# Attention of a first block regrouped over head pairs, and its first projections loaded raw through SyncE's queue

## The chip, the core and the metric

The kernel runs on one core of a Trainium2 chip. The metric is the device time of one execution in microseconds. The core has five instruction streams that this document names: TensorE (PE, matmuls; PEld is its weight load), VectorE (DVE), ScalarE (ACT), GpSimd (POOL, which here mostly issues DMAs) and SyncE (SP, which only issues DMAs). Matmuls read SBUF and write PSUM, which is held as eight buffers of 128 x 512 floats.

## The reference

The reference runs a two-layer "first block" and then a two-layer second block on 512 tokens of width 1024. Only the first block is touched. Cut to what matters, one layer of it is:

```
h = rmsnorm(x) ; z = h @ w_in                 # 1024 -> 1280 columns: fourier, 8 q heads, 2 k, 2 v heads, 4 memory q heads
y_f = real(fft2(z_fourier)) @ w_fourier       # 256 columns
q, k = rope(zq), rope(zk)
y_a = softmax(q k^T / 8 + window mask, with a sink logit) @ v      # |i - j| <= 128, 8 heads on 2 kv heads
km, vm = split(rmsnorm(mem) @ w_mem_kv)       # 256 memory tokens
y_m = softmax(zm km^T / 8) @ vm               # 4 heads
y = concat(rmsnorm(y_f), rmsnorm(y_a), rmsnorm(y_m)) @ w_out
x = x + rmsnorm(y)
x = x + rmsnorm((silu(h2 @ w_gate) * (h2 @ w_up)) @ w_down)        # h2 = rmsnorm(x), width 2816
```

All of it is in float32. The kernel gets float32 accuracy from fp32r matmuls by splitting each operand into a rounded high part and a remainder.

## The kernel before, in words

**Data.** Activations are feature-major: a tile holds 128 features by 512 tokens. A product of split operands is three matmuls (`mm3`, line 713: high times low, low times high, high times high). A weight tile of 1024 x 128 is loaded in two halves of 128 x 512 (`halves`, line 692): a DMA on POOL's queue writes the rounded high part, an engine writes its negative (`scale` by -1), and a second DMA on POOL's queue adds the original to it, so that the remainder is left. One output tile of a projection is 8 `mm3`, 24 matmuls of 512 columns. Everything in SBUF that matters here takes one of 100 slots of 128 x 512 floats (`NSLOT`), and a PSUM tile takes one of the eight buffers.

**The order of instructions** is worked out on the host. The program first records every operation in program order (`Plan.record`); `Plan.schedule` (line 423) then places them on the five engines by a model of their durations: each engine takes, of the operations that the model says are ready, the one that is needed earliest in TensorE's program order, up to 120 us ahead. Transfers are modelled as one queue in which all DMAs run one after the other (`state["dma"]`, lines 569 to 576). Each engine then runs its list strictly in that order on the chip. An operation that opens a tile earlier than program order would is only placed if no point of the program in between is filled up (`room`, line 465; `load` counts the tiles that are live at each point of the program order, and `self.low` is the first operation not yet placed):

```
if op.index > self.low and load[k][self.low:op.index].max() + n > self.cap[k] - min(self.MARGIN.get(k, 0), int(ahead / self.PACE)):
    return False
```

For PSUM the cap is 8 and the margin 0.

**A layer of the first block** (`block1`, line 1107) does this. `enter` (line 838) splits the eight tiles of x, times the gain, into high and low parts and sums their squares; the norm's factor itself (`late`, the tile `rb`) is worked out behind the first four projections and multiplied into their results. The ten projections (`project`, by `linear`, line 734) are recorded as tiles 4 (k), 0 (q), 5 (v), 1 (q) first, then 2 and 3, 6 and 7, 8 and 9 between the attention parts (0 to 3 are pairs of q heads, 6 and 7 the memory queries, 8 and 9 the fourier part). A tile below 5 gets rope in `ev` (line 1112): four DMAs on SP's queue shift blocks of 32 partitions, and three VectorE operations combine the tile with its shifted copy.

The attention of a head (`attend`, line 1064) has two parts. The first writes four score tiles (a block of 128 queries each, against two or three blocks of keys; two of 256 and two of 384 columns), three matmuls each with a contraction of 64, and the softmax on them. The second transposes the probabilities 128 x 128 at a time through TensorE, splits them, and multiplies them with the values. `run` (line 1159) records the first part of both heads of a pair, then a set of projections, then the second parts of both heads. Memory attention follows for its two pairs. After it, `group` normalises the three groups, each before its split, the fourier group last and by the other form of norm (`wide`, line 819), and the output projection runs its eight tiles one after another, 24 matmuls each.

In layer 0 `mem_in`, `mem_k`, `mem_v` (memory norm, keys and values) and `four_fold` (a small product of the channel transform with the fourier weights) are recorded between these parts; for layer 1 memory keys and values are worked out around layer 0's feed-forward part. In the first layer `linear` runs the four first projections one after the other; in the second it runs them in two halves of the tokens (`first=4`).

## Time and profile before

| | us |
|---|---|
| median of 3 runs | 3524.22 |
| lowest, highest | 3521.81, 3525.62 |
| the profiled execution | 3527.36 |
| its span (first to last instruction) | 3525.2 |
| TensorE busy in it | 3446.0 |

The profile is of one execution. TensorE's column counts a matmul as busy from its issue to its modelled end, at either clock, so 98% busy doesn't say that it ran at its full rate. Every operation has the line 646, because the plan issues them all from there; they are told apart by their tiles: `ps` is PSUM, `s` the slots, `in_...` tensors in memory. The shape of a matmul is written as contraction*columns of the stationary operand, then the moving operand: `128*128 128x512` is a projection, `64*128 64x256` a score tile, `128*64` a product with the values, and `ident` marks a transpose.

### The profile page before, as it was taken

The numbers are of one execution on the slowest core, as the hardware profiler recorded it, in microseconds if no ns is written. First come the engines' busy times: TensorE is split into PE (matmuls) and PEld (weight loads), VectorE is DVE, ScalarE is ACT, GpSimd is POOL, SyncE is SP. The second block draws the span as 40 slices with busy tenths as digits, with TensorE's granted clock in tenths as the row PEclk, the third lists the DMA queues.
The fourth block names the chain that finished last, engine by engine and source line by source line (L and its number), as shares of the span: only waits on it lengthen the run. The fifth ranks groups of instructions, "written<-read, shape, count | busy, mean of one in ns | idle before, by whom it ended". The sixth has DMA issues, their size and how long they took to land.

```text
span 3525.2 us, 44631 instructions
## 1 busy us (share of the span) xinstructions
PE 3446.0 (98%) x16280; PEld 2869.9 (81%) x16280; DVE 1941.6 (55%) x3942; ACT 882.9 (25%) x1709; POOL 1756.8 (50%) x2447
## 2 busy tenths in 40 slices
PE   7899999889999999999999999999999999999998
PEld 6688888768888988887888888888888888888887
DVE  6875432687342553339997444335333899844332
ACT  3642000364000211015733110011001574411000
POOL 5155454535446464653365544655465436654462
PEclk9899999889999999999999999999999999999999
DMA  9278797848779797996699977999799769998794
GB/s 251 60 175 192 158 202 153 202 105 172 165 156 218 170 218 162 220 218 128 131 220 229 235 158 158 216 198 203 159 215 218 139 121 228 214 238 170 161 199 107
DMA packets 361596, 638.02 MB, mean 181 GB/s; under 512 B 40736, under 2 KB 64032, under 8 KB 361376
## 3 DMA queue, kind: packets, MB, share of 16 engines
q0 software_dynamic: 349056, 616.75, 81.8%
q1 hardware_dynamic: 12320, 18.42, 1.6%
q8 instruction: 128, 2.10, 0.2%
q14 instruction: 92, 0.75, 0.1%
HBM read 626.10 MB, written 6.29 MB: 179 GB/s over the span
## 4 chain that ended last, share of the span: by engine, by line
PE 91%; DVE 4%; DMA 2%; issue 2%; ACT 0%; POOL 0%; SPq 0%; POOLq 0%; DVEq 0%; ACTq 0%
PE ps L646 91%; DVE s L646 4%; DMA s<-in_b_in 1%; ACT s L646 0%; POOL s L646 0%; DMA s<-in_a_in 0%; DMA s<-in_c_chan 0%; DMA s<-in_x 0%; DVE mx L646 0%; POOL rinv L646 0%; DVE sp L646 0%; SPq L646 0%; DVE rc L646 0%; DVE nb L646 0%; DVE sums L646 0%
## 5 line engine op out<-in xcount | busy, mean ns | idle before, releaser
L646 PE MATMUL ps<-s 128*128 128x512 f32 (+2 forms) x15706 | 3381.5, 376 | 45.2 <-DVE s L646 26.2
L646 PEld LDWEIGHTS ps<-s 128*128 128x128 f32 (+1 forms) x15706 | 2796.3, 188 | 602.9 <-issue 30.5
L646 POOL DMA_DIRECT2D s<-in_b x1088 | 786.3, 1028 | 667.9 <-DVE s L646 296.6
L646 ACT ACTIVATE s<-s 128x512 fp32r<-128x512 f32 (+3 forms) x716 | 404.6, 601 | 1737.5 <-DVE s L646 1128.4
L646 DVE TENSOR_TENSOR s<-ps,s 128x512 f32<-128x512 f32 (+4 forms) x642 | 397.8, 636 | 637.5 <-PE ps L646 631.8
L646 DVE TENSOR_SCALAR s<-s 128x512 fp32r<-128x512 f32 (+2 forms) x845 | 341.3, 423 | 471.5 <-DMA s<-in_b 278.5
L646 POOL DMA_DIRECT2D s<-in_a_f x544 | 396.9, 1082 | 348.4 <-DVE s L646 163.2
L646 DVE TENSOR_TENSOR s<-s 128x512 f32<-128x512 f32 (+2 forms) x822 | 500.3, 624 | 54.8 <-ACT s L646 33.3
L646 POOL DMA_DIRECT2D s<-in_b_in x368 | 287.8, 1008 | 266.7 <-ACT s L646 88.7
L646 DVE SCALAR_TENSOR_TENSOR s<-s,vecs 128x256 fp32r<-128x256 f32 (+25 forms) x446 | 287.9, 678 | 6.3 <-ACT s L646 3.2
L646 ACT ACTIVATE s<-s,vecs 128x512 f32<-128x512 f32 (+2 forms) x213 | 135.7, 656 | 310.2 <-DVE s L646 297.4
L646 POOL DMA_DIRECT2D s<-in_a_out x64 | 48.5, 994 | 156.5 <-PE ps L646 100.7
L646 DVE SCALAR_TENSOR_TENSOR s<-ps,s 128x512 f32<-128x512 f32 (+1 forms) x33 | 22.2, 674 | 183.0 <-PE ps L646 183.0
L646 ACT ACT_TABLE_LOAD x67 | 86.0, 1283 | 55.8 <-DVE s L646 47.9
L646 ACT ACTIVATE s<-ps 128x512 f32<-128x512 f32 (+1 forms) x40 | 21.3, 534 | 269.2 <-PE ps L646 245.7
L646 PE MATMUL ps<-ident,s 128*128 128x128 f32 x392 | 68.9, 307 | 20.0 <-DVE s L646 14.4
L646 DVE RECIPROCAL s<-s 128x128 f32<-128x128 f32 (+1 forms) x48 | 83.1, 1741 | 8.3 <-ACT s L646 8.2
L646 DVE CAST s<-s 128x512 fp32r<-128x512 f32 (+1 forms) x190 | 81.9, 431 | 6.8 <-DMA s<-in_pos 1.2
L646 ACT ACTIVATE s<-s,nb 128x256 f32<-128x256 f32 (+3 forms) x128 | 70.5, 552 | 44.9 <-DVE nb L646 43.4
L646 PEld LDWEIGHTS ps<-ident,s 128*128 128x128 f32 x392 | 53.0, 157 | 33.8 <-DVE s L646 15.3
L646 POOL TENSOR_TENSOR rinv<-rms,nhalf 128x2 f32<-128x2 f32 (+1 forms) x17 | 17.3, 1015 | 117.0 <-DVE rms L646 109.0
L646 POOL DMA_DIRECT2D s<-in_a_in x80 | 58.8, 884 | 24.9 <-DMA s<-in_a_in 13.1
(71 smaller groups left out, 874.1 us busy)
## 6 DMA issues: line engine op xcount, KB each, us to landing
s<-in_b POOLq DMA_DIRECT2D x1024, 256.0 KB, 6.5
s<-in_a_f POOLq DMA_DIRECT2D x512, 256.0 KB, 6.3
s<-in_b_in POOLq DMA_DIRECT2D x368, 256.0 KB, 6.4
s<-in_a_in POOLq DMA_DIRECT2D x80, 256.0 KB, 7.6
s<-in_a_out POOLq DMA_DIRECT2D x64, 256.0 KB, 7.4
s<-in_b_out POOLq DMA_DIRECT2D x64, 256.0 KB, 7.6
s<-in_b POOLq DMA_DIRECT2D x64, 128.0 KB, 6.3
s<-in_b_mo POOLq DMA_DIRECT2D x32, 256.0 KB, 5.9
```

Of the source, the lines that this page charges most:

```text
L646: getattr(getattr(nc, op.eng), op.fn)(*[real(v) for v in op.args], **{k: real(v) for k, v in op.kw.items()})
```

## The change

Five things change in the first block.

1. Attention is recorded as separate steps for a pair of heads: `scores` writes the eight score tiles of both heads, alternating between the heads matmul by matmul; `turn` transposes and splits one head's probabilities; `apply` multiplies with the values. `ask(p)` is scores and softmax of pair p, `answer` is `turn`, `put` is `apply`. Scores of pair p+2 are recorded behind the last product of pair p. Pairs 4 and 5 are the memory heads.
2. The other matmuls (projections 2, 3, 6, the memory keys and values in layer 0, projections 7, 8, 9, `four_fold`, fourier) are a generator, `fillers`, from which `pull(us)` records a given amount of TensorE work between the steps. It stops right behind a matmul, so that a projection's PSUM tile can be open, its evacuation not yet recorded, when the next step is recorded.
3. In layer 0 the first four projections are recorded by `open`: raw float32 halves come by one DMA each on SP's queue and are split by ScalarE or VectorE; all four tiles take contraction steps 0 to 3 first and 4 to 7 after that.
4. The three group norms all use the form with the narrow sums (`inv` and `bcast`), in steps (`Group`) that are recorded apart.
5. The output projection opens five tiles at once, over the window heads' four steps first, then the fourier steps, then the memory steps; the other three tiles follow as before.

`mem_k`, `mem_v` and `fourier` become generators that yield between their matmuls; the plan, its model and its limits are as before.

```diff
+    def scores(self, heads, rng):
+        mm = self.nc.tensor.matmul
+        S = [[] for _ in heads]
+        for i in range(4):
+            a, b = rng[i]
+            cols, kc = slice(128 * i, 128 * i + 128), slice(128 * a, 128 * b)
+            for t in S:
+                t.append(self.ps()[:, :128 * (b - a)])
+            for n, (x, y) in enumerate(((0, 1), (1, 0), (0, 0))):
+                for t, (q, k, (lo, hi)) in zip(S, heads):
+                    mm(t[i], q[x][lo:hi, cols], k[y][lo:hi, kc], start=n == 0, stop=n == 2)
+        return S
...
+    def turn(self, P, rng, order):
+        nc = self.nc
+        out = []
+        for kb in order:
+            qs = [i for i in range(4) if rng[i][0] <= kb < rng[i][1]]
+            q0, q1 = 128 * qs[0], 128 * (qs[-1] + 1)
+            pt = self.ps()[:, :q1 - q0]
+            for j, i in enumerate(qs):
+                off = 128 * (kb - rng[i][0])
+                nc.tensor.transpose(pt[:, 128 * j:128 * j + 128], P[i][:, off:off + 128], self.ident)
+            h, l = self.t(F32R)[:, :q1 - q0], self.t(F32R)[:, :q1 - q0]
+            self.split(pt, h, l)
+            out.append((kb, slice(q0, q1), h, l))
+        return out
...
+    def apply(self, turned, V, vcols, y, yrows):
+        po = self.ps()[0:64]
+        for n, (kb, q, h, l) in enumerate(turned):
+            self.mm3(po[:, q], V[0][kb][:, vcols], V[1][kb][:, vcols], h, l, n == 0, n == len(turned) - 1,
+                     skip_group_check=True)
+        self.nc.copy(y[yrows[0]:yrows[1]], po)
...
+    def steps(self, srcs, acts, evac):
+        kt = len(acts)
+        for m, src in enumerate(srcs):
+            ps = self.ps()
+            w = {}
+            for k in range(kt):
+                if k // 8 not in w:
+                    w[k // 8] = self.wload(src[k // 8])
+                wh, wl = w[k // 8]
+                self.mm3(ps, wh[:, k % 8], wl[:, k % 8], acts[k][0], acts[k][1], k == 0, k == kt - 1)
+                yield 0.68
+            evac(m, ps)
+    def open(self, srcs, acts, evac):
+        nc = self.nc
+        pss = [self.ps() for _ in srcs]
+        for c in (0, 4):
+            for m, src in enumerate(srcs):
+                raw, h, l = (self.t(dt).rearrange("p (k c) -> p k c", c=128) for dt in (F32, F32R, F32R))
+                nc.sync.dma_start(out=raw, in_=src[0][:, c:c + 4])
+                self.split(raw, h, l)
+                for k in range(4):
+                    self.mm3(pss[m], h[:, k], l[:, k], acts[c + k][0], acts[c + k][1],
+                             c + k == 0, c + k == KD - 1)
+        return lambda: [evac(m, ps) for m, ps in enumerate(pss)]
...
+    class Group:
+        def __init__(self, net, l, ys, ks, acts):
+            self.net, self.l, self.ys, self.ks, self.acts = net, l, ys, ks, acts
+            self.s = net.squares(ys)
+        def rms(self):
+            self.r = self.net.inv([self.s], 128 * len(self.ys))
+        def finish(self):
+            net = self.net
+            rb = net.bcast(self.r)[1]
+            for k, y in zip(self.ks, self.ys):
+                net.tt(y, rb, out=y)
+                self.acts[k] = net.split_gain(y, net.vec(f"g_grp{self.l}", k))
...
-        project([4, 0, 5, 1], hold=4, before=late, first=4 if l else 0)
+        src = lambda ms: [[I[f"a_in{l}"][m]] for m in ms]
+        ms = [4, 0, 5, 1]
+        if l == 0:
+            done = self.open(src(ms), a, lambda i, ps: ev(ms[i], ps))
+            late()
+            done()
+        else:
+            self.linear(src(ms), a, lambda i, ps: ev(ms[i], ps), hold=4, before=late, first=4)
...
+        near = [(0, 2), (0, 3), (1, 4), (2, 4)]
+        every = [(0, 2)] * 4
...
-        run(window(0, ya[0]), lambda: project([2, 3]))
-        if l == 0:
-            self.mem_in()
-        run(window(1, ya[1]), lambda: project([6, 7]))
-        run(window(2, ya[2]), lambda: project([8, 9]))
-        if l == 0:
-            self.four_fold()
-        run(window(3, ya[3]), lambda: (self.mem_k(0), self.mem_v(0)) if l == 0 else None)
-        run(memory(0, ym[0]))
-        run(memory(1, ym[1]))
-        acts = []
-        def group(ys):
-            rb = self.norm(ys, 128 * len(ys), wide=self.W[1 + len(acts) // 3])
-            for y in ys:
-                self.tt(y, rb, out=y)
-                acts.append(self.split_gain(y, self.vec(f"g_grp{l}", len(acts))))
-        group(ya)
-        group(ym)
-        group(self.fourier(l, [z[8], z[9]]))
+        acts = {}
+        def fillers():
+            rest = [2, 3, 6]
+            yield from self.steps(src(rest), a, lambda i, ps: ev(rest[i], ps))
+            if l == 0:
+                self.mem_in()
+                yield 0.0
+                yield from self.mem_k(0)
+                yield from self.mem_v(0)
+            last = [7, 8, 9]
+            yield from self.steps(src(last), a, lambda i, ps: ev(last[i], ps))
+            if l == 0:
+                self.four_fold()
+            yield from self.fourier(l, [z[8], z[9]])
+        fill = fillers()
...
+        def pull(us):
+            for cost in fill:
+                us -= cost
+                if us <= 0:
+                    break
+        def ask(p):
+            if p < 4:
+                S = self.scores([(z[p], z[4], r) for r in rows], near)
+                return [self.softmax(S[u], 0.125, (self.vec(f"sink{l}", p + 4 * u), nsink[:, p + 4 * u:p + 4 * u + 1]),
+                                     mask) for u in range(2)]
+            t = p - 4
+            S = self.scores([(z[6 + t], self.km[t], r) for r in rows], every)
+            return [self.softmax(S[u], 0.125) for u in range(2)]
+        def answer(p, P, u):
+            if p < 4:
+                return self.turn(P[u], near, [0, 3, 1, 2])
+            return self.turn(P[u], every, [0, 1])
+        def put(p, turned, u):
+            if p < 4:
+                self.apply(turned, z[5], slice(64 * u, 64 * u + 64), ya[p], rows[u])
+            else:
+                hd = 2 * (p - 4) + u
+                self.apply(turned, self.vm, slice(64 * hd, 64 * hd + 64), ym[p - 4], rows[u])
+        P = {0: ask(0)}
+        pull(5.4)
+        P[1] = ask(1)
+        pull(5.4)
+        groups = {}
+        for p in range(6):
+            t0 = answer(p, P[p], 0)
+            if p == 4:
+                groups[0] = self.Group(self, l, ya, range(4), acts)
+            pull(1.3)
+            t1 = answer(p, P[p], 1)
+            if p == 4:
+                groups[0].rms()
+            put(p, t0, 0)
+            pull(1.3)
+            if p == 4:
+                groups[0].finish()
+            put(p, t1, 1)
+            if p < 4:
+                P[p + 2] = ask(p + 2)
+                pull(3.3 if l else 5.3)
+            del P[p]
+        pull(100.0)
+        groups[1] = self.Group(self, l, self.yf, (6, 7), acts)
+        groups[2] = self.Group(self, l, ym, (4, 5), acts)
         ev, post = self.keep(f"g_post{l}")
-        self.linear([[I[f"a_out{l}"][m]] for m in range(KD)], acts, ev, last=2, done=post)
+        outs = [I[f"a_out{l}"][m] for m in range(KD)]
+        n = 5
+        first = [0, 1, 2, 3]
+        w = [self.wload(outs[m]) for m in range(n)]
+        full = [self.ps() for _ in range(n)]
+        def add(m, ks):
+            for k in ks:
+                self.mm3(full[m], w[m][0][:, k], w[m][1][:, k], acts[k][0], acts[k][1], k == 0, k == 5)
+        for m in range(n):
+            add(m, first)
+            if m == 1:
+                groups[1].rms()
+                groups[2].rms()
+            if m == 2:
+                groups[1].finish()
+                groups[2].finish()
+        for m in range(n):
+            add(m, [6, 7])
+        for m in range(n):
+            add(m, [4, 5])
+            ev(m, full[m])
+        self.linear([[outs[m]] for m in range(n, KD)], [acts[k] for k in range(KD)],
+                    lambda m, ps, c=ALL: ev(m + n, ps, c), last=2, done=post)
...
@@ mem_k and mem_v: after each mm3 @@
+                yield 0.36
@@ fourier: after each token block, and after each table of a token block @@
+            yield 0.7
...
-        return ys
+        self.yf = ys
```

## Rows read from the trace of the kernel before

**Rows 1.** The page: span, TensorE's busy time, and the chain that ended last.
```profile
span 3525.2 us, 44631 instructions
PE 3446.0 (98%) x16280; PEld 2869.9 (81%) x16280; DVE 1941.6 (55%) x3942; ACT 882.9 (25%) x1709; POOL 1756.8 (50%) x2447
...
PE 91%; DVE 4%; DMA 2%; issue 2%; ACT 0%; POOL 0%; SPq 0%; POOLq 0%; DVEq 0%; ACTq 0%
```
**Rows 2.** Windows by stage: start:end, length, busy us (instructions), clock, DMA share, GB/s.
```profile
0.00:22.09 22.09, 0.79 (x1) 0.32 (x2) 12.38 (x25) 11.12 (x17) 11.11 (x24) 1.00 1.01 308
20.00:46.00 26.00, 23.91 (x98) 20.23 (x99) 25.34 (x47) 10.60 (x16) 19.28 (x26) 1.00 1.18 289
31.40:83.90 52.50, 52.36 (x237) 43.26 (x236) 30.31 (x55) 10.62 (x21) 26.48 (x34) 1.00 1.05 236
83.90:198.20 114.30, 94.88 (x564) 75.43 (x565) 99.13 (x288) 72.46 (x202) 29.74 (x47) 0.87 0.34 78
620.70:652.60 31.90, 28.45 (x209) 27.59 (x208) 22.67 (x63) 10.66 (x28) 24.62 (x35) 0.89 1.12 271
652.60:685.60 33.00, 33.00 (x148) 27.06 (x147) 16.68 (x23) 9.33 (x14) 19.11 (x25) 1.00 1.14 254
685.60:788.70 103.10, 84.23 (x472) 65.38 (x472) 89.89 (x253) 62.50 (x177) 28.14 (x45) 0.82 0.40 90
```
**Rows 3.** Windows of the stretches in which the granted clock fell, one per layer.
```profile
83.90:143.00 59.10, 44.26 (x224) 33.31 (x224) 50.26 (x158) 35.16 (x98) 1.65 (x4) 0.77 0.05 14
685.60:738.20 52.60, 37.78 (x175) 30.01 (x174) 42.39 (x126) 24.08 (x70) 2.66 (x5) 0.64 0.17 41
```
**Rows 4.** Timeline of the start: start, length, instructions, idle before and its releaser.
```profile
15.05 0.72 ACT L646 ACTIVATE s<-s,first 128x512 fp32r<-128x512 f32 x1 [0.94 <-DMA s<-in_x]
22.09 9.06 PE L646 MATMUL ps<-s 128*128 128x64 f32 x31 [13.30 <-DMA s<-in_c_chan]
```
**Rows 5.** Timeline of VectorE and SyncE's queue around the ropes of both layers.
```profile
44.42 1.89 DVE L646 TENSOR_TENSOR s<-ps,s 128x512 f32<-128x512 f32 x3
45.14 2.53 SPq L646 DMA_DIRECT2D s<-s  x4
50.80 2.42 SPq L646 DMA_DIRECT2D s<-s  x4
73.58 2.02 DVE L646 TENSOR_TENSOR s<-s 128x512 f32<-128x512 f32 x3
...
661.60 3.08 DVE L646 TENSOR_TENSOR s<-ps,s 128x512 f32<-128x512 f32 x5
662.43 18.59 SPq L646 DMA_DIRECT2D s<-s  x20
687.36 2.01 DVE L646 TENSOR_TENSOR s<-s 128x512 f32<-128x512 f32 x3
```
**Rows 6.** DMA issues of the rope's shifts: count, KB each, median us to landing.
```profile
s<-s SPq DMA_DIRECT2D x40, 64.0 KB, 6.4
```
**Rows 7.** The loads of x: issue time ns (min/median/max), first and last start us.
```profile
L646 SPq DMA_DIRECT2D s<-in_x x8: 418/444/804, 1.2 to 5.0; - x8
```
**Rows 8.** Groups on VectorE in the first 46 us: splits of a 512-wide half.
```profile
L646 DVE TENSOR_SCALAR s<-s 128x512 fp32r<-128x512 f32 x12 | 4.9, 429 | 4.0 <-DMA s<-in_a_in 4.0
L646 DVE TENSOR_TENSOR s<-s 128x512 fp32r<-128x512 f32 x2 | 1.4, 687 | 0.0
```
**Rows 9.** Groups on TensorE by form: a projection's matmul, busy and mean ns.
```profile
L646 PE MATMUL ps<-s 128*128 128x512 f32 x13210 | 3027.7, 390 | 8.4 <-DVE s L646 8.4
```
**Rows 10.** Timeline of score matmuls: eight and three of one head; ten, partly two heads.
```profile
164.94 1.22 PE L646 MATMUL ps<-s 64*128 64x256 f32 x8
165.75 0.98 PE L646 MATMUL ps<-s 64*128 64x256 f32 x10
766.80 0.62 PE L646 MATMUL ps<-s 64*128 64x256 f32 x3
```

More of the change, by code (lines that the diff above doesn't have):

```diff
@@ L1129, in ev @@
                 z[m] = self.split_t(t)
-        def project(ms, **k):
-            self.linear([[I[f"a_in{l}"][m]] for m in ms], a, lambda i, ps: ev(ms[i], ps), **k)
-        project([4, 0, 5, 1], hold=4, before=late, first=4 if l else 0)
+        src = lambda ms: [[I[f"a_in{l}"][m]] for m in ms]
[6 more added lines that the diff above has]
+            self.linear(src(ms), a, lambda i, ps: ev(ms[i], ps), hold=4, before=late, first=4)
         nsink = self.small(8, "nsink")
         nc.vector.tensor_scalar(out=nsink, in0=self.vec(f"sink{l}"), scalar1=-1.0, scalar2=None, op0=ALU.mult)
-        rng = [(0, 2), (0, 3), (1, 4), (2, 4)]
+        near = [(0, 2), (0, 3), (1, 4), (2, 4)]
+        every = [(0, 2)] * 4
         win = self.t()[:, :384]
@@ L1142, in block1 @@
         mask = [win[:, 128:384], win, win, win[:, 0:256]]
-        def window(t, y):
-            for u in range(2):
-                hd = t + 4 * u
-                rows = (64 * u, 64 * u + 64)
-                yield self.attend(z[t], z[4], rows, rng, 4, z[5], slice(64 * u, 64 * u + 64), 0.125, y, rows,
-                                  sink=(self.vec(f"sink{l}", hd), nsink[:, hd:hd + 1]), mask=mask,
-                                  order=[0, 3, 1, 2], starts=(0,))
-        def memory(t, y):
-            for u in range(2):
-                rows = (64 * u, 64 * u + 64)
-                hd = 2 * t + u
-                yield self.attend(z[6 + t], self.km[t], rows, [(0, 2)] * 4, 2, self.vm,
-                                  slice(64 * hd, 64 * hd + 64), 0.125, y, rows, starts=(0,))
@@ L1159, in run @@
-        def run(gens, *between):
-            gens = list(gens)
-            for g in gens:
-                next(g)
-            for b in between:
-                b()
-            for g in gens:
-                for _ in g:
-                    pass
+        rows = [(0, 64), (64, 128)]
         ya = [self.t() for _ in range(4)]
         ym = [self.t() for _ in range(2)]
-        run(window(0, ya[0]), lambda: project([2, 3]))
-        if l == 0:
-            self.mem_in()
-        run(window(1, ya[1]), lambda: project([6, 7]))
@@ L1194, in block1 @@
         more = l + 1 < self.nl1
         if more:
-            self.mem_k(l + 1)
+            for _ in self.mem_k(l + 1):
+                pass
         ev, post = self.keep(f"g_pff{l}")
@@ L1199, in block1 @@
         if more:
-            self.mem_v(l + 1)
+            for _ in self.mem_v(l + 1):
+                pass
     def mem_in(self):
@@ L1253, in mem_v @@
                 self.mm3(ps, hs[k][:, tok], ls[k][:, tok], wh, wl, k == 0, k == KD - 1)
+                yield 0.36
             self.split(ps, vh[:, NMEM * j:NMEM * j + NMEM], vl[:, NMEM * j:NMEM * j + NMEM])
@@ L1302, in fourier @@
                     self.mm3(po[j][tab], vs[tb][0][:, c], vs[tb][1][:, c], h, l_, tb == 0, tb == 3)
+                yield 0.7
         ys = []
```

## Prediction

> **What bounds the kernel now.** I read the page first. TensorE is busy 98% of a span of 3525.2 us and 91% of the chain that ended last is its own [rows 1], so outside the first block nothing but fewer matmuls would help, and the change doesn't touch anything there. Then I cut the first block into windows [rows 2], looking for stretches with little busy time or a clock under 1.00. There are five. From 0 to 22.09 TensorE does one matmul. From 31.4 to 83.9 it is dense: these are the projections, all ten of them, since the plan drew the later six ahead while the first scores weren't ready. From 83.9 to 198.2 (layer 0, first score to first matmul of the output projection) it is busy 94.88 of 114.3 us, at 0.87 of the clock, with VectorE at 99.13. In layer 1 the same three stages are 620.7 to 652.6 (first four projections), 652.6 to 685.6 (the other six, no gap) and 685.6 to 788.7, busy 84.23 of 103.1 at 0.82, with VectorE at 89.89 and ScalarE at 62.50. So in the attention stages TensorE waits for softmax and split, and part of what looks busy is slow. The third look is at where the clock falls [rows 3]: mean 0.77 over 59.1 us and 0.64 over 52.6 us. With two levels, 1.2 and 2.4 GHz, that is 27 us and 38 us at the low one; TensorE is busy there 75% and 72%, so 20 and 27 us of its busy time ran at half rate, and 10.2 and 13.6 us of it are lost.
>
> I count in the time of the profiled execution: 3527.4 us, 2.2 above its span, 3.1 above the median of the runs.
>
> **The opening.** Before, TensorE's first long run begins at 22.09, behind 13.30 us of waiting for a constant of `four_fold`, which the plan had put first [rows 4]. In the new program order that product comes behind projection 9, so I take it that it no longer leads. But the start doesn't set the end of this stage; the rope does. Rows 5 show layer 0: VectorE evacuates the first projections at 44.42, when the norm's factor is there. Four shift DMAs of tile 4 are issued at 45.14 and of tile 0 only at 50.80, since VectorE waits there for TensorE; with 2.42 us of issue and a median of 6.4 us to land [rows 6], tile 0's shifted copy is there at about 59.6. Yet VectorE combines it at 73.58, because its list has evacuations of later projections ahead, and scores begin at 83.9. So 14 us lie between data and use.
>
> After the change, SP's queue carries x and the raw halves, 16 DMAs of 256 KB instead of 8. The eight of x are issued from 1.2 us on [rows 7] and ScalarE waits for the last until 15.05 [rows 4]: 13.9 us for 2.1 MB while POOL's queue loads beside it. At that pace the last raw half lands at 29; with its split and 12 matmuls the four projections end at 33 us (19 if SP had the 308 GB/s of rows 2 to itself, 50 if as before). On VectorE each raw half costs a copy of 0.43 and a subtraction of 0.69 [rows 8], 8 x 1.1 = 9 us if all stay there; eight splits of the old kind (0.43 each, 3.4 us) go. VectorE is full from 20 to 46 (25.34 of 26 us) [rows 2], so the norm's factor comes 0 to 6 us later; I take 3: 47. Evacuation of tiles 4 and 0 follows together (1.3), then 8 shift issues (5), 6.4 to land, 2.0 of rope and 1.1 of split: scores begin at about 62. The bounds are 57 (no delay of the factor) and 72 (the plan's model, in which shifts queue behind weight loads, puts the rope late again).
>
> **What fills the gap.** Here I choose against the change. `scores` opens eight PSUM tiles before any is drained, and the cap is eight. By the quoted condition of the plan, an operation that opens a PSUM tile may not be placed ahead of a point where the live count plus its own exceeds 8. Before, no point had more than about five, so the six projections could slip in front of the scores. Now every `ask` is a wall: nothing recorded behind it that needs PSUM starts before it. So TensorE idles from 33 to 62 in layer 0, and in layer 1 from 652.6 until its first scores. There the evacuations start at 661.60, the 20 shift issues take 0.93 us each from 662.43, so tiles 4 and 0 are issued by 669.9 and landed by 676; rope and split 3 us, 679; I take 680 (674 if tile 0's shifts land as soon as issued, 687 if the list order is as before, where VectorE combined them at 687.36) [rows 5]. The six projections then stand inside attention, where TensorE was slow and waiting.
>
> **Work from the first score on.** Layer 1: 84.23 busy, less 13.6 lost to the clock, 70.6. Add six projections of 24 matmuls at 3027.7 / 13210 = 0.229 us [rows 9]: 33.0. Take off what the alternation saves: three scores of one head take 0.62 us and eight 1.22, so each further one adds 0.12; ten, the later ones from two heads in turn, take 0.98, so the seven beyond three add 0.05 each: two run at a time [rows 10]. A layer has 96 score matmuls of 256 columns (0.12) and 48 of 384 (0.18): 20 us, of which half can go; a little alternates already, so 8.5. That leaves 95 us. VectorE and ScalarE have 89.89 + 62.50 = 152, plus some 15 for evacuating projections that used to come earlier, 84 each if shared evenly [rows 2]: under 95, so TensorE sets the pace, but not by much. Layer 0: 94.88 - 10.2 + 33.0 - 8.5 + 2.5 for `four_fold` = 112.
>
> On top comes friction. A row shows what a change of form costs: of the 0.62 us of three scores that stand alone [rows 10], 0.36 is their pace and 0.16 the way from pace to end of the last (0.390 less 0.229 for a wide one, rows 9), which leaves 0.10 for the first. Pieces of projections between the steps add some four changes per pair, 24 a layer: 2.4 us. The rest of friction is the tail of each barrier (below); I take 6 us in layer 0, where the memory's norm, split and keys hang on one another, and 4 in layer 1 (0 and 20 as bounds). The Trainium skill ("TensorEngine Tiling (Array Packing)", section "Key Properties") says that changing the tiling mode, and not just the tile, drains TensorE. By that every entry into a 64-row score group and every exit pays; counted for all eight changes per pair it would be 4.8 us a layer, and the sum 5 us higher. The 0.10 us agrees with a short drain on entry.
>
> The norm that changes form drops a long reciprocal on VectorE; it and the narrow norms lie beside the 60 matmuls (13.7 us) with which five output tiles begin, so I count nothing, and 3 us if that cover fails. The five tiles want 20 slots of weights at once; DMA share in the attention stages was 0.34 and 0.40 [rows 2], so the bandwidth is there, but slots are held longer (split x until projection 9). I add 1 us of waiting per layer, 0 to 8.
>
> **The sum.** Layer 0: 62 + 112 + 6 = 180 instead of 198.2, 18 earlier. Layer 1: 680 + 95 + 4 = 779 instead of 788.7, 10 earlier. Less 2: 26 us. 3527.4 - 26 = 3501 in the profiled execution's terms, 3498 against the median.
>
> **Rivals.**
> *The gaps are short and attention flows.* Scores at 57 and 674, no friction, output weights in time: 57 + 112 = 169 and 674 + 95 = 769, 29 and 20 earlier; 49 in all, 3475. For it: shifts are on the chip well before they were used [rows 5]. Against: VectorE and ScalarE at 84 of 95 us leave no slack for a bad order.
> *The fillers still run ahead of the scores.* If my reading of the wall is wrong, TensorE does the six projections in the gap as before, and attention is set by VectorE and ScalarE as now. Then layer 0 starts its scores some 14 us earlier, layer 1 gains the 4 or 5 us by which alternating scores shorten steps that wait: 18 in all, 3506. Against: the count of eight is plain in the new program.
> *The walls cost more than the holes they fill: slower.* A half-done projection is open when an `ask` is recorded, so the live count is nine there; the last score tile, and all PSUM work behind it, must wait until everything recorded earlier has been placed: softmax, rope, memory split. There are five such walls a layer. If each stops TensorE for 3 us beyond my friction, 30 us go and the gain is used up; at 7 us (a softmax of four tiles, or the landing of a shift, 6.4) it is 70 us, 3568; half of them at that price, 3535. For it: the lists are in order, and VectorE and ScalarE are nearly full. Against: a pair's softmax has a whole pair of steps, 95 / 6 = 16 us, to finish.
>
> **How the numbers follow.** The forecast (3498, own range 3480 to 3515) gets 0.45, flowing attention (3475) 0.22, fillers ahead (3506) 0.15, walls (3535) 0.18. A measurement of this kernel can't tell less than 0.2%, 7 us, from no change: 3517 to 3531. Faster: 0.45 less a little, 0.22, most of 0.15: 0.76. Same: 0.11, from the upper edges and the cheaper walls. Slower: 0.13. The range 3454 to 3534 leaves out the far ends of the walls and, below, a case where flowing attention also shortens the DMA-bound stretch at 620.7 to 652.6.
>
> **What would show it.** Right: no matmuls between about 33 and 60, and again from 653 to about 678; scores in runs at 0.06 us each; 512-column matmuls inside attention, the clock at 1.00 there; pairs some 16 us apart; the first output matmul at about 180 and 780. Wrong: dense projections before the first score (no wall), idle TensorE in front of each pair's last score tile (walls too dear), or waits for `in_a_out` or `in_a_f` behind attention (slots).

## The result, and the profile after

The changed kernel takes 3481.03 us (median of four runs, 3480.19 to 3482.72) against 3524.92 (3521.81 to 3527.34) of the kernel before on the same chip: ratio 0.9877, 95% interval 0.9859 to 0.9894, 43.9 us less. The forecast was 3498, 26 less. The direction and the range held; the gain is two thirds larger than forecast.

The page of the kernel after, the lines that answer to [rows 1]:

```profile
span 3479.6 us, 44666 instructions
PE 3404.2 (98%) x16296; PEld 2844.1 (82%) x16296; DVE 1923.0 (55%) x3916; ACT 893.1 (26%) x1732; POOL 1748.9 (50%) x2433
```

The span is 45.6 us shorter and TensorE's busy time 41.8 us shorter (3446.0 less 3404.2), with about as many matmuls (16296, before 16280). So the gain is hardly idle time that went away: the same work took less time. The windows of the stages say where. Of the kernel after, with the columns of [rows 2]: the gap of layer 0 (from the end of the first projections to the first scores, where TensorE has almost nothing to do), its attention, then the gap and attention of layer 1.

```profile
33.50:58.30 24.80, 1.85 (x7) 1.02 (x8) 22.74 (x38) 9.22 (x12) 4.07 (x4) 0.58 0.60 111
58.30:173.90 115.60, 107.50 (x720) 91.57 (x721) 104.96 (x298) 86.05 (x233) 40.64 (x59) 0.97 0.58 125
631.90:644.80 12.90, 0.17 (x2) 0.00 (x0) 6.57 (x11) 1.11 (x2) 4.17 (x6) 0.61 1.28 267
644.80:740.60 95.80, 92.67 (x602) 77.89 (x603) 86.74 (x250) 67.44 (x189) 39.56 (x58) 0.96 0.63 131
```

Now the same two pieces of work in both kernels: from the start to the first matmul of layer 0's output projection, and from the end of layer 0's MLP to that of layer 1's. (Layer 1's first such matmul before is at 787.3; it hides in a longer group of the timeline, and the prediction's 788.7 is the next group.) Before:

```profile
0.00:198.20 198.20, 157.34 (x833) 127.14 (x834) 151.03 (x385) 100.04 (x249) 75.47 (x114) 0.92 0.65 157
620.60:787.30 166.70, 144.38 (x822) 119.20 (x822) 128.07 (x336) 81.19 (x217) 70.57 (x102) 0.87 0.69 158
```

After:

```profile
0.00:173.90 173.90, 134.46 (x822) 111.42 (x823) 147.17 (x369) 112.34 (x272) 59.42 (x90) 0.92 0.68 160
599.40:740.70 141.30, 120.99 (x815) 104.75 (x814) 122.33 (x326) 82.41 (x223) 68.12 (x100) 0.93 0.80 175
```

Layer 0 is 24.3 us shorter and layer 1 25.4; the stretch between them is 3.1 longer (425.5 for 422.4), and all behind it 1.0 longer: 45.6. The stretch between is longer because matmuls of the last two group norms now stand behind the mark: it holds 2127 matmuls instead of 2107, 2.2 us more of busy time, and 0.9 us more of waiting. Subtract busy from length in each row: TensorE is idle 40.9 us before and 39.4 after in layer 0, 22.3 and 20.3 in layer 1. It waits as long as before. Its busy time fell by 22.9 and 23.4 us, some 2 of these 46 because narrow sums of the norms moved behind the two marks.

Two things made most of it fall. First the clock: the attention stages went from 0.87 and 0.82 [rows 2] to 0.97 and 0.96. The low stretches now lie mostly in the gaps (0.58 and 0.61), where there are 1.85 and 0.17 us of matmuls to slow down; the 38 us of layer 1 and 27 of layer 0 at 1.2 GHz used to lie on work [rows 3]. In layer 0 the mean clock of the whole piece is 0.92 in both kernels: it spends about as long at 1.2 GHz as before (32 and 28 us, from these means), but with little to do. Slow work shows in the transposes of layer 0's attention before, by form (columns of [rows 9]), from 83.9 to 143, where the clock fell, and from 143 to 185, where it was 1.00:

```profile
L646 PE MATMUL ps<-ident,s 128*128 128x128 f32 x60 | 12.9, 358 | 11.3 <-DVE s L646 7.3 <-ACT s L646 4.1
...
L646 PE MATMUL ps<-ident,s 128*128 128x128 f32 x44 | 6.5, 279 | 0.5 <-ACT s L646 0.3
```

That is 0.215 us of busy time for one in the first stretch and 0.148 in the second; in the kernel after it is 0.130 (14.6 us for 112, a row further down). The first difference goes with the clock, the second doesn't: at full clock, too, a transpose costs somewhat less in the new order. How the two divide over all forms no run separates. Second the scores, by form, columns of [rows 9], in the attention stage of layer 0. Before:

```profile
L646 PE MATMUL ps<-s 64*128 64x256 f32 x96 | 15.7, 311 | 0.2
...
L646 PE MATMUL ps<-s 64*128 64x384 f32 x48 | 12.2, 372 | 0.0
```

After:

```profile
L646 PE MATMUL ps<-s 64*128 64x256 f32 x96 | 10.9, 310 | 8.2 <-DVE s L646 7.4 <-DVE mx L646 0.8
...
L646 PE MATMUL ps<-s 64*128 64x384 f32 x48 | 6.3, 378 | 0.0
```

The mean length of one (310 and 378 ns) hasn't moved, but their busy time fell from 27.9 to 17.2 us: two run at a time. The run without pairs (below) divides the 46 us: 31 had gone there, and pairs take the other 15.

How the gap looks, TensorE's timeline of the kernel after (columns of [rows 4]), layer 0 and then layer 1:

```profile
12.91 20.59 PE L646 MATMUL ps<-s 128*128 128x512 f32 x87 [0.19 <-ACT s L646]
...
49.79 1.11 PE L646 MATMUL ps<-ident,s 128*128 128x128 f32 x4 [12.67 <-DVE s L646]
58.30 2.16 PE L646 MATMUL ps<-s 64*128 64x256 f32 x12 [7.39 <-DVE s L646]
...
621.19 0.63 PE L646 MATMUL ps<-s,onesr 128*128 128x512 f32 x2
621.66 9.98 PE L646 MATMUL ps<-s 128*128 128x256 f32 x82
...
644.87 1.52 PE L646 MATMUL ps<-s 64*128 64x256 f32 x8 [12.79 <-DVE s L646]
```

And what fills the gap, VectorE and SP's queue, the answer to [rows 5] (in layer 1 the issues begin at 630.17):

```profile
47.85 2.49 DVE L646 TENSOR_TENSOR s<-ps,s 128x512 f32<-128x512 f32 x4
48.62 7.58 SPq L646 DMA_DIRECT2D s<-s  x12
52.64 2.02 DVE L646 TENSOR_TENSOR s<-s 128x512 f32<-128x512 f32 x3 [0.33 <-DMA s<-s]
...
629.34 1.89 DVE L646 TENSOR_TENSOR s<-ps,s 128x512 f32<-128x512 f32 x3
...
639.22 2.02 DVE L646 TENSOR_TENSOR s<-s 128x512 f32<-128x512 f32 x3 [5.74 <-DMA s<-s]
```

Before, 29 us passed in layer 0 from evacuating (reading a finished result out of PSUM) to combining the rope (44.42 to 73.58) and 26 in layer 1 (661.60 to 687.36); now it is 4.8 and 9.9. Nothing of later projections stands between them on VectorE.

### The profile page after: what moved, and what is told of

Same layout as the page of the kernel before. It is cut to its first block, busy times and chain, and to the rows that moved or that the text cites. A ratio compares the mean times of both kernels' runs of the same rounds, so it can differ in the third digit from the quotient of the medians.

```text
span 3479.6 us, 44666 instructions
## 1 busy us (share of the span) xinstructions
PE 3404.2 (98%) x16296; PEld 2844.1 (82%) x16296; DVE 1923.0 (55%) x3916; ACT 893.1 (26%) x1732; POOL 1748.9 (50%) x2433
## 4 chain that ended last, share of the span: by engine, by line
PE 90%; DVE 4%; DMA 2%; issue 1%; ACT 1%; POOL 1%; SPq 0%; POOLq 0%; DVEq 0%; ACTq 0%
PE ps L646 90%; DVE s L646 4%; ACT s L646 1%; DMA s<-in_x 1%; POOL s L646 0%; DMA s<-in_b_in 0%; DMA s<-in_pos 0%; DMA s<-in_a_in 0%; DMA s<-s 0%; POOL rinv L646 0%; DVE mx L646 0%; DMA s<-in_a_out 0%; DMA s<-in_a_mk 0%; SPq L646 0%; DVE sp L646 0%
## 5 line engine op out<-in xcount | busy, mean ns | idle before, releaser
L646 ACT ACTIVATE s<-s 128x512 fp32r<-128x512 f32 (+2 forms) x702 | 396.9, 601 | 1713.0 <-DVE s L646 1142.4
L646 DVE SCALAR_TENSOR_TENSOR s<-ps,s 128x512 f32<-128x512 f32 (+1 forms) x33 | 22.3, 674 | 187.2 <-PE ps L646 187.0
L646 DVE CAST s<-s 128x512 fp32r<-128x512 f32 x192 | 83.8, 436 | 6.5 <-DMA s<-in_pos 1.1
L646 POOL DMA_DIRECT2D s<-in_a_in x64 | 47.2, 931 | 76.2 <-DVE s L646 24.4
L646 PE MATMUL ps<-ident,s 128*128 128x128 f32 x392 | 56.7, 275 | 14.2 <-DVE s L646 14.2
L646 ACT CAST s<-ps 128x256 fp32r<-128x256 f32 (+4 forms) x142 | 59.9, 455 | 34.0 <-PE ps L646 28.5
```

The lines of the kernel that those rows point to most:

```text
L646: getattr(getattr(nc, op.eng), op.fn)(*[real(v) for v in op.args], **{k: real(v) for k, v in op.kw.items()})
```

## The experiments

All of them compute the whole reference. Theory: the wall, that is, scores that open eight PSUM tiles against the cap of eight, keeps the later projections behind the first scores, and this pays twice, by an early rope and by an attention without holes. Rivals: the pairing of heads, the raw opening, the depth of two pairs, or the opening of the output carries the gain. Ratios are to the kernel before, timed in the same job, that is, beside it on the same chip. Counted in the recorded programs, the kernel before never has more than 5 PSUM tiles live; the changed one reaches 8 at the first set of scores of a layer and 9 at the other five.

**The changed kernel again, beside the first experiments.** No edit.

> The changed kernel again, as the base of this series: 3481 us (3477 to 3485), 44 below the kernel before.

3483.83 us, 0.9882 (0.9868 to 0.9895). This is the reference for what follows.

**Matmuls of one head in a block.**

```diff
-            for n, (x, y) in enumerate(((0, 1), (1, 0), (0, 0))):
-                for t, (q, k, (lo, hi)) in zip(S, heads):
+            for t, (q, k, (lo, hi)) in zip(S, heads):
+                for n, (x, y) in enumerate(((0, 1), (1, 0), (0, 0))):
```

> The changed kernel, but the score matmuls of a pair go head by head instead of alternating; still eight tiles open, so the wall stands. Theory (TensorE sets attention's pace, so what alternation saves on it is gained): 8.5 us a layer are lost, 3498 us (3494 to 3501). Rival (VectorE and ScalarE set the pace, TensorE has slack there): 3481 to 3486 us.

3479.65 us, 0.9870 (0.9857 to 0.9884): nothing lost. But it took no pairs away either. The scores of layer 0's attention in this run:

```profile
L646 PE MATMUL ps<-s 64*128 64x256 f32 x96 | 11.2, 309 | 7.6 <-DVE s L646 7.4 <-ACT s L646 0.2
...
L646 PE MATMUL ps<-s 64*128 64x384 f32 x48 | 6.5, 381 | 0.0
```

17.7 us, near the 17.2 with turns by matmul: blocks of three still ran in pairs. So this run says nothing on what pairing is worth; the next one does.

**All of one head's scores, then all of the other's.** Eight tiles are still opened together, so the wall stands.

```diff
-        for i in range(4):
-            ...
-            for t in S:
+        for t, (q, k, (lo, hi)) in zip(S, heads):
+            for i in range(4):
```

> The changed kernel with all twelve score matmuls of a pair's first head recorded ahead of the second head's, both softmaxes behind; eight tiles stay open (the wall stands), but matmuls of two heads no longer stand within three of one another, so that they should run one at a time (0.12 us for 256 columns instead of 0.06). Theory of the prediction (TensorE sets attention's pace): 8 to 10 us a layer are lost, 0.993 to 0.994 of the kernel before, about 3500 us. Rival (VectorE and ScalarE keep TensorE waiting by as much anyway): within 5 us of the changed kernel, 0.988 to 0.990, 3484 to 3489.

3492.33 us, 0.9901 (0.9888 to 0.9915). A kernel of the same job that keeps the pairs (the opening of the output, below) took 3485.85, so pairing is worth 6.5 us. The scores of layer 0, and the two pieces of work:

```profile
L646 PE MATMUL ps<-s 64*128 64x256 f32 x96 | 14.9, 312 | 7.4 <-DVE s L646 7.4
L646 PE MATMUL ps<-s 64*128 64x384 f32 x48 | 11.6, 384 | 0.0
...
0.00:178.30 178.30, 142.34 (x823) 118.27 (x824) 148.25 (x374) 111.28 (x267) 59.34 (x90) 0.91 0.66 156
603.60:749.80 146.20, 128.15 (x815) 111.82 (x814) 123.42 (x327) 81.98 (x223) 68.28 (x100) 0.93 0.79 168
```

Pairs save 9.3 us of scores in layer 0 (26.5 against 17.2). TensorE's busy time differs by 7.9 and 7.2 us, but idle time comes back in exchange (36.0 here, 39.4 with pairs in layer 0; 18.0 and 20.3 in layer 1). Where TensorE is faster it waits longer: behind the gap, its waits in layer 0's attention are 4.8 us here and 8.1 with pairs, nearly all for VectorE and ScalarE.

**Four tiles open instead of eight: no wall.** Scores of one head, its softmax, then the other head.

```diff
-                S = self.scores([(z[p], z[4], r) for r in rows], near)
-                return [self.softmax(S[u], 0.125, ..., mask) for u in range(2)]
+                return [self.softmax(self.scores([(z[p], z[4], rows[u])], near)[0], 0.125, ...,
+                                     mask) for u in range(2)]
```

> As the run without alternation, and the softmax of the first head is recorded ahead of the second head's scores, so that only four score tiles are open at any point and there is no wall. Theory of the prediction (the wall costs the gap ahead of the first scores): TensorE does projections in the gap and the time is 10 to 25 us below the run without alternation. Rival (the wall is what keeps the projections for attention, where TensorE would else wait): the gap is filled, attention thins out as before the change, and the time is equal to the run without alternation or up to 20 us above it.

3503.91 us, 0.9937 (0.9925 to 0.9950), 20.1 us more than the changed kernel beside it. It lacks the pairs as well; against the run without pairs (0.9901) the wall alone is worth 0.0036, 13 us. Its windows: from the opening to the scores, attention, and the two pieces of work.

```profile
36.70:69.30 32.60, 22.89 (x95) 18.59 (x95) 23.12 (x37) 8.19 (x11) 5.36 (x6) 0.87 0.58 128
69.30:185.10 115.80, 105.95 (x630) 90.79 (x631) 102.18 (x294) 85.53 (x230) 37.98 (x57) 0.86 0.50 103
...
0.00:185.10 185.10, 154.57 (x822) 128.66 (x823) 147.60 (x371) 112.36 (x270) 58.17 (x90) 0.89 0.62 147
610.50:763.70 153.20, 134.92 (x810) 113.19 (x809) 121.00 (x325) 80.58 (x221) 68.53 (x103) 0.92 0.73 168
```

Projections do fill the gap (22.89 of 32.60 us busy), and layer 0 is idle 30.5 us only, less than the 36.0 with the wall. Yet it ends later: busy time is 12.2 us more in layer 0 and 6.8 in layer 1, with the attention at 0.86 instead of 0.97. The wall is worth more than the idle time it makes.

**The wall alone, on the kernel before.** Both heads' scores are recorded ahead of the first softmax, so eight tiles are open; nothing else of the change. The count of live tiles is 8 at six points of each layer.

```diff
             S.append(ps)
+        if apart:
+            yield
         P = self.softmax(S, scale, sink, mask)
...
-            for g in gens:
-                next(g)
+            for _ in range(2):
+                for g in gens:
+                    next(g)
```

> The kernel before with one thing changed: of a pair, both heads' scores are recorded ahead of both softmaxes, so that eight tiles are open and projections recorded behind them can't run ahead (the wall), two of them inside each of the first three pairs as the old program has them; nothing of the new steps, no alternation, old opening, old norms. Theory (the wall, which keeps projections beside softmax, is what the change gained most by): 10 to 25 us below the kernel before, 0.993 to 0.997. Rival (the wall is only good with scores recorded two pairs ahead): no gain or a loss, 1.000 to 1.010.

3501.06 us, 0.9925 (0.9913 to 0.9937): 26 us, the largest part of those tried alone. The windows of its attention and of its two pieces of work:

```profile
61.50:185.10 123.60, 119.80 (x729) 102.78 (x730) 104.49 (x297) 78.33 (x216) 40.93 (x59) 0.94 0.55 117
...
0.00:185.10 185.10, 148.17 (x831) 124.32 (x832) 146.29 (x373) 106.80 (x263) 78.17 (x115) 0.92 0.74 173
607.10:759.60 152.50, 131.45 (x824) 112.35 (x823) 125.04 (x331) 85.69 (x225) 72.75 (x106) 0.94 0.79 174
```

Scores begin at 61.5 instead of 83.9. Of the 27.3 us by which the two pieces are shorter than before, 22.1 are busy time and 5.2 idle. To the changed kernel (0.9882) another 15 us are left; the pairs are 6.5 of them, and no run adds the rest (the second pair ahead, the smaller pieces of other matmuls, the form of the group norms) to the wall one by one. Layer 1 shows one more thing. Its norm's factor is on VectorE when the evacuation starts; in this run:

```profile
635.74 1.89 DVE L646 TENSOR_TENSOR s<-ps,s 128x512 f32<-128x512 f32 x3
```

and without a wall (the run with four tiles open):

```profile
650.06 3.08 DVE L646 TENSOR_TENSOR s<-ps,s 128x512 f32<-128x512 f32 x5
```

Counted from the end of layer 0's MLP (607.1 and 610.5) that is 28.6 and 39.6 us; 29.9 in the changed kernel and 41.0 before. Where the wall stands the factor is there 11 us earlier. In the changed kernel its two matmuls stand at 621.19, ahead of the last 82 matmuls of the first four projections; before, behind them:

```profile
642.26 10.09 PE L646 MATMUL ps<-s 128*128 128x256 f32 x82 [0.22 <-DMA s<-in_a_in]
652.18 0.63 PE L646 MATMUL ps<-s,onesr 128*128 128x512 f32 x2
```

Why the plan's list draws them ahead was not tried.

**Projections drawn into the gap on purpose.** Once 5.4 us ahead of the first scores in both layers, once 16.3 in layer 0 and 5.4 in layer 1.

```diff
+        pull(5.4)                  # and: pull(5.4 if l else 16.3)
         P = {0: ask(0)}
```

> The changed kernel with one projection recorded ahead of the first scores in both layers, in the gap where TensorE waits for the rope (25 us in layer 0, 13 us in layer 1). Theory (TensorE sets the pace of attention, so what it does in the gap is gained): 5.5 us a layer, 11 in all, 0.985 of the kernel before, 3473 us. Rival (VectorE sets the pace, 103 of 115.6 us busy in attention of layer 0): 0 to 4 us, 3480 to 3484.

3487.41 us, 0.9889 (0.9876 to 0.9903).

> As the run with one projection ahead, but three in layer 0 (2, 3 and 6). Theory (TensorE sets the pace): 16.5 and 5.5 us, 22 in all, 0.982 of the kernel before, 3462 us. Rival (attention without its projections leaves TensorE waiting for softmax again): no gain beyond the run with one ahead, or a loss of up to 10 us, 3473 to 3494.

3497.80 us, 0.9917 (0.9904 to 0.9931): 1.6 and 12.0 us more than the 3485.85 of the same job. The 1.6 is within the spread of the runs (3486.73 to 3490.61 against 3483.77 to 3487.09), so one projection ahead gains nothing, and three lose. The second one's windows in layer 0:

```profile
33.00:71.20 38.20, 22.15 (x82) 17.15 (x80) 30.95 (x53) 15.57 (x26) 11.29 (x14) 0.80 0.81 156
71.20:182.40 111.20, 97.26 (x657) 83.50 (x658) 100.16 (x291) 78.08 (x217) 39.56 (x59) 0.88 0.53 117
```

With 22 us of projections in the gap, the scores begin 12.9 us later (71.2), attention is only 4.4 us shorter, idle 13.9 us instead of 8.1, and at 0.88. VectorE shows why the scores are late: it waits 4.75 us for TensorE to finish the last of the drawn-in projections, and the splits that the first scores read come behind that evacuation.

```profile
63.78 0.69 DVE L646 TENSOR_TENSOR s<-ps,s 128x512 f32<-128x512 f32 x1 [4.75 <-PE ps L646]
```

Here a projection is worth more between two steps of attention than in an empty gap.

**One pair ahead instead of two.**

```diff
-        pull(5.4)
-        P[1] = ask(1)
-        pull(5.4)
+        pull(10.8)
...
+            if p < 5:
+                P[p + 1] = ask(p + 1)
             if p < 4:
-                P[p + 2] = ask(p + 2)
```

> The changed kernel with scores recorded one pair ahead of their use instead of two (same fillers between). Theory (two pairs ahead hide a pair's softmax, some 8 us from its first score to its last scaled probability): about 3 us per pair come back, 30 us in all, 0.996 to 0.998 of the kernel before. Rival (the projections between the steps hide it alone): within 5 us of the changed kernel, 0.988 to 0.990.

3508.22 us, 0.9949 (0.9935 to 0.9963): 0.0067, 24 us, above the changed kernel. Window of attention in layer 0 and the transposes by form:

```profile
62.40:186.00 123.60, 112.38 (x721) 97.19 (x722) 107.83 (x305) 82.99 (x219) 42.98 (x63) 0.92 0.52 105
...
L646 PE MATMUL ps<-ident,s 128*128 128x128 f32 x112 | 17.2, 298 | 6.0 <-ACT s L646 6.0
```

After (same form, its attention in layer 0):

```profile
L646 PE MATMUL ps<-ident,s 128*128 128x128 f32 x112 | 14.6, 273 | 1.5 <-DVE s L646 1.5
```

The transposes, which read the softmax, wait 6.0 us for ScalarE instead of 1.5 for VectorE, and the clock is 0.92: a softmax doesn't fit behind one pair's work alone. Not all of the 24 us is that: the first scores of layer 0 also begin 4.1 us later (62.4 for 58.3).

**The raw opening: taken out of the changed kernel, and put alone into the kernel before.**

```diff
-        if l == 0:
-            done = self.open(src(ms), a, lambda i, ps: ev(ms[i], ps))
-            late()
-            done()
-        else:
-            self.linear(..., hold=4, before=late, first=4)
+        self.linear(..., hold=4, before=late, first=4 if l else 0)
```

> The changed kernel with the opening of layer 0 as before (weights in two passes on GpSimd's queue, tile after tile). Theory (the rope, not the projections, sets when the first scores begin, and the constant for four_fold no longer leads): within 5 us, 3476 to 3486. Rival (the raw loads bring the earlier start): the first scores begin 10 to 16 us later, 3491 to 3497 us.

3484.56 us, 0.9885 (0.9870 to 0.9900), the same as with it. VectorE combines the rope 2.6 us earlier than with the raw opening (50.03 for 52.64).

The second edit is the reverse: `open` of the change is copied into the kernel before and used for layer 0.

> The kernel before with the raw opening of layer 0 alone. Theory (the first scores wait for the rope, which VectorE's list puts behind evacuations of later projections, whatever the opening): within 6 us of the kernel before, 0.998 to 1.002. Rival (the earlier end of the first projections is worth the 14 us between rope data and use): 0.995 to 0.996.

3510.87 us, 0.9956 (0.9943 to 0.9968): 16 us, as the rival had it. In its profile layer 0's MLP ends 13.8 us earlier (606.8 for 620.6) and layer 1 is 4.0 shorter. (The first matmul of the output projection is no mark here: it comes 19.4 us earlier, but ahead of 42 of the 48 fourier matmuls of 258 columns.) TensorE's timeline begins with one long run (7.81 to 33.47), and the product of `four_fold` (by form) has no idle time ahead of it:

```profile
L646 PE MATMUL ps<-s 128*128 128x64 f32 x16 | 2.1, 274 | 0.0
```

So alone it removes the 13.30 us wait for `in_c_chan` [rows 4]. The wall alone, and the old opening in the changed kernel, have no such wait either. The two gains overlap, 26 and 16 don't add up, and in the changed kernel the wall has already taken it.

**The output projection tile by tile.**

```diff
+        for g in (1, 2):
+            groups[g].rms()
+            groups[g].finish()
+        self.linear([[I[f"a_out{l}"][m]] for m in range(KD)], [acts[k] for k in range(KD)], ev, last=2, done=post)
```

(in place of the five tiles opened at once)

> The changed kernel with the output projection's eight tiles one after another and the last two group norms recorded ahead of it. Theory (the 60 matmuls on the window heads' part cover the norms): 4 to 8 us a layer are lost, 0.991 to 0.993 of the kernel before, 3492 to 3500 us. Rival (the plan hides the norms in some other way): within 4 us, 0.988 to 0.9895.

3485.85 us, 0.9882 (0.9869 to 0.9896): no difference. Five tiles at once are worth nothing here.

**A narrow first norm.** The long reciprocal of 3.35 us ahead of the evacuation gives way to the form with narrow sums.

```diff
-            self.rb = self.wide([s], D)
+            self.rb = self.bcast(self.inv([s], D))[1] if narrow else self.wide([s], D)
```

> The changed kernel with the narrow form for the first norm of both layers (four narrow sums, a power on GpSimd and a broadcast product instead of the wide product, a root and a reciprocal of 3.35 us on VectorE). Theory (the chain from the norm to the rope sets the gap, 22 us in layer 0 and 13 us in layer 1): 4 to 6 us in layer 0, 3 to 4 in layer 1, 8 in all, 0.986 of the kernel before. Rival (the shifts' landing sets the gap): within 3 us of the changed kernel, 0.9875 to 0.989.

3487.13 us, 0.9887 (0.9873 to 0.9900). The scores of layer 0 start 3.2 us earlier (55.05 for 58.30), but layer 1's start 47.4 us behind layer 0's MLP, 1.9 later than the changed kernel's, its attention is 3.4 longer, and in sum nothing is won. No run beats the changed kernel by more than the intervals.

## Why the prediction was right, and where it was off

*The opening: right.* Predicted 33, measured 33.5; the factor predicted at 47, evacuation at 47.85. Scores at 58.3 instead of 62: the shifts take 0.63 us each to issue (7.58 for 12) as assumed, but they land in 2.0 us and not in 6.4 (last section), so VectorE combines 4.0 us after the first issue. Against that, from there to the scores 5.7 us pass and not 3.1, since the two tiles' ropes and splits follow one another on VectorE. Also right is that the rope and not the start sets the end of this stage: without the raw opening the scores start no later.

*What fills the gap: right, and worth more than I gave it.* Eight tiles against a cap of eight do keep every projection behind the scores, in both gaps as foretold. The prediction had the gap as the price of an early rope and a denser attention, and put the kernel without it ("fillers run ahead") 8 us above the forecast, 3506 against 3498. Without the wall it is 13 us slower where neither kernel has pairs, and the wall alone is worth 26 on the kernel before. What the price step missed is that the wall moves the norm's factor in layer 1 too (next point). "Against the change" was the mistaken phrase: with one projection drawn into the gap nothing was gained and with three 12 us were lost, so it isn't spare time.

*Layer 1's scores: the term that was mis-sized.* Predicted 680, 59.4 us behind layer 0's MLP; measured 45.5. The 13.9 us are the largest part of the error. I had left the evacuation where it was before (661.60 [rows 5]), 41.0 us behind the MLP. The wall changes its place too: 29.9. The rest of that step was sound: 18.4 us predicted from evacuation to scores, 15.5 measured.

*Work from the first score on: right to 3%.* Attention in layer 0, predicted 112 and 6 of friction, is 115.6; in layer 1, predicted 95 and 4, it is 95.8. Busy alone: 107.5 for 112 and 92.7 for 95. The clock came back to 0.97 and 0.96, not to the 1.00 of the sum: the first scores still run at the low level that begins in the gap (0.60 from 58.3 to 62). So the sum had other parts of the work too long.

*Alternation: its matmul time right, its worth not.* The term of 8.5 us a layer measures 9.3 of matmul time in layer 0, but 6.5 us for both layers in the end, for 17. TensorE's busy time is 15.1 us less than without pairs, and 5.7 of that come back as idle time, most of it waits for VectorE and ScalarE (105 and 86 us busy of 115.6). The sum hid this error since the idle time in attention that goes with it was in "friction". And no alternation by matmul is needed; blocks of three do as well.

*Friction and forms.* TensorE's waits inside attention of layer 0, in the kernel after: us in total, times, longest:

```profile
PE ps L646 <- DVE s L646: 9.9, 4, 7.4
PE ps L646 <- DVE mx L646: 2.9, 3, 2.0
PE ps L646 <- ACT s L646: 2.4, 1, 2.4
PE ps L646 <- PE ps L646: 0.3, 1, 0.3
```

The longest, 7.4, is the end of the gap before the first score. What is left is 8.1 us in eight waits, against 6 of friction; in layer 1 it is 3.1 against 4. None waits for a DMA, so the five output tiles' slots held nothing up there; nor does any from there to the end of layer 0's MLP. What a change of form costs no run measured by itself; the rule of the Trainium skill ("TensorEngine Tiling (Array Packing)", "Key Properties"), by which the prediction had 5 us more, is neither shown nor refuted.

*Edits costed at nothing.* The output's opening is confirmed by its run: 0. The group norms' new form has no run of its own; what shows of it are the 20 matmuls and 0.9 us of waiting behind the mark, so the cover very nearly held.

*The sum.* The error of 19.6 us in the span (45.6 less 26): layer 0's scores 3.7 and attention 2.4 earlier; layer 1's scores 13.9 and attention 3.2; the 2 us taken off for slots didn't show; against it 4.1 lost between and behind the two layers and 1.4 from the mark at 788.7. Together 19.7. Of the 4.1, 3.1 are the group norms' matmuls and waits behind the first mark (above), so its mark makes layer 0 look somewhat shorter than it became.

*Rivals.* "Fillers run ahead" is excluded by the gap, "walls too dear" by waits of 8.1 and 3.1 us in attention and since the runs without the wall are the slower ones. "Flowing attention" (3475) is the nearest in number; its scores at 57 come close to 58.3, but its layer 1 at 674 still has the late factor, so it comes near the time in part for another reason: that 3475 is nearer to 3481 than the forecast is partly luck.

## What to carry to other kernels

Before filling an idle gap with other matmuls, ask what those matmuls' evacuations stand in front of, and where the low clock would then fall: in this kernel an idle stretch with nothing in it was cheaper than the same idle time spread through dense work. So compare busy time and idle time of the same piece of work in both kernels, not lengths of stages; here idle time stayed at 40 and 21 us, and nearly the whole gain was busy time. A limit on open tiles is a scheduling tool: it moved everything behind it, including a norm's product, which no edit had touched, eleven microseconds earlier.

## What was not expected of the hardware

Two heads' score matmuls on different 64 rows ran in pairs though three of one head stood in front of each three of the other: 17.7 us of busy time for 144, against 17.2 in strict turns and 26.5 with twelve in a block. The Trainium skill ("TensorEngine Tiling (Array Packing)", "Key Properties") says that different tiles can run matmuls at the same time; the trace agrees. It shows more. These are the score matmuls that have begun within 0.12 us of a pair's first, with blocks of three (from 86.08) and then with blocks of twelve (from 88.33):

```profile
L646 PE MATMUL ps<-s 64*128 64x256 f32 x2 | 0.4, 384 | 0.0
...
L646 PE MATMUL ps<-s 64*128 64x256 f32 x1 | 0.4, 384 | 0.0
```

Matmuls of one head follow one another more slowly than that (second row), so with blocks of three the second that has begun must be the other head's, though the other two of the first head stand ahead of it in TensorE's list. So here a matmul on the other 64 rows starts ahead of two that wait.

The rope's shifts, 64 KB each, took as long to issue in both layers of the kernel after (median 0.59 us), but not to land. From issue to landing of the first 12, us, least, median and most, in layer 0 and then in layer 1:

```profile
DMA to landing us min/median/max: 1.9/2.0/2.0
...
DMA to landing us min/median/max: 5.5/6.4/7.0
```

The DMA share of these stretches was 0.34 (48.0 to 56.2) and 1.23 (630 to 640). VectorE waited 0.33 us for a shift in layer 0 and 5.74 in layer 1, so the slower landing may cost some 5 us of layer 1's gap. That the other traffic is what slows it was not shown by a run of its own.
